# A decoder block on one core: the first expert pairs directly behind the routing choice, half of the embedding and the shared expert inside the first groups of four, a group of four at the end

## The chip, the core and the metric

The kernel runs on one core of one Trainium2 chip. The metric is the time of one execution on the device, in microseconds (us). TensorE is called PE in the profile (PEld is its weight load), VectorE DVE, ScalarE ACT, GpSimd POOL. SyncE (SP) issues nearly all loads; "SPq" is its queue.

## What is computed

One layer: 256 tokens of width 1024 go through two mixing branches (dilated attention and a gated recurrence) and a first norm, which gives `x1`. The change touches only what comes after that:

```python
idx, gate = route(h, w_router, bias)       # sigmoid scores, 4 of 8 expert groups, 8 of 64 experts per token
y_moe = (routed_experts(h, idx, gate, expert_w_gate, expert_w_up, expert_w_down)
         + swiglu(h, shared_w_gate, shared_w_up, shared_w_down))
ple = jax.nn.sigmoid(x1 @ ple_gate_w) * (p @ ple_proj_w)
x = layer_norm(ALPHA * x1 + y_moe + ple, ln2_w, ln2_b)
```

All 64 experts get some tokens, so all 64 sets of weights are read: three tiles of 128 x 2048 float32 (1 MB, 1,048,576 bytes) for each expert, 192 tiles in all. The embedding's gate weights (`pleg`) are four such tiles, the shared expert's gate and up (`shgu`) two, its down (`shd`) one.

## The kernel before, in words

**Stages.** Up to the first norm, PE works through the projections, the attention and the recurrence. Then (L596 to L620) `x1` is transposed and split in a high and a low part (`x1h`, `x1l`), and `dense` (L576) multiplies it with a weight in eight chunks of 128 rows. For each chunk ACT makes the high part of the weight, DVE the low part (`w2h`, `w2l`, W2 = 3 buffers of each), and PE does six matmuls of 512 columns.

**The choice.** The router's logits go through PE, ACT and then a chain of small DVE operations (L652 to L685) that ends in the mask `em`; `place` (L691) makes each token's slot (`posm`) of it with three matmuls and two DVE operations. While DVE works on this chain, PE runs `gated[0]` and `gated[1]`, the two halves of the embedding's gate (eight chunks each); DVE makes their low parts in between.

**Between the choice and the experts.** After `place`, PE runs the shared expert's gate and up (`shared`, eight chunks), and between the chunks come `add_emb` (L816, which puts the embedding and the residual into the accumulators `acc`) and the pieces of `rank` (L706), which orders the experts 8 to 63 by their load and writes the list `ids`. Experts 0 to 7 are in fixed order (FIXED = 8). SP reads `ids` before it loads any later expert (`expert_at`, L825).

**The experts.** `units` (L799) lists 13 units of two groups each. A group is a pair of experts (64 slots each) or four experts (32 slots each, the 24 experts with the fewest tokens; SMALL_AT = (2, 6, 9) says which units these are). For a group, PE gathers the tokens with a one-hot matrix `sel` (`unit`, `gather`, four steps for one unit's two groups, `xe`), multiplies with gate and up (tiles n = 0 and n = 1 of each expert), waits for `swiglu`, transposes `h`, multiplies with down (n = 2) and adds to `acc` (`scatter`). The gather steps of the next unit, and the second half of the scatter of the group before, are filled in between; two gather steps in each group.

**The ring.** All weight tiles go through a ring of slots of 1 MB (`slot`, L72), in order. RING_A 9, RING_B 6, RING_X 2 and the buffer of `x1` make 18; two more (RING_C) are added when the buffers of `dense` are given back, ahead of the first unit. A load waits until PE or DVE has read the tile that its slot held, and SP issues loads strictly in order, at most eight at a time in flight.

**The end.** The last unit's weights come in halves of 512 KB. Then the last norm (L1005) and the output.

PE's matmuls stand in the written order from L598 on (`fixed["pe"]`); DVE operations stand in it only where `late` holds them; the rest is ordered by the scheduler when the kernel is built.

Of the kernel before, what the change touches and what calls it, by code (L numbers as in the profile page):

```python
# [18 lines left out]
S = 256  # L19
# [3 lines left out]
NE = 64  # L23
# [9 lines left out]
WARM, YB, TB, W2 = 8, 2, 2, 3  # L33
FIXED, SMALL, SMALL_AT = 8, 24, (2, 6, 9)
# [3 lines left out]
RANK_AT = (1, 2, 3, 5)  # L38
# [18 lines left out]
def tile_block(ctx: ExitStack, tc: tile.TileContext, a, out: bass.AP):  # L57
# [50 lines left out]
    ple = ExitStack()  # L108
    ptg = ple.enter_context(tc.tile_pool(name="ptg", bufs=1))
# [304 lines left out]

    def gates():
        gp = transposed(next_win())
        t = ptg.tile([128, 2, S], F32, name="tg", bufs=4)
        act.activation(t, gp, AF.Tanh, scale=0.5)
        return t
# [97 lines left out]
    for f in range(2):  # L517
        if f:
            ps = [pmx.tile([128, 512], F32, name="ah", bufs=2) for _ in range(2)]
        else:  # L520
            ps = [ppj.tile([128, 512], F32, name="pj", tag="pj") for _ in range(2)]
        for i in range(2):
            for kt in range(2):
                whi, wlo = (w[f] for w in pws[kt])
                ts = slice(256 * kt + 128 * i, 256 * kt + 128 * i + 128)
                mm(ps[i], phi[:, ts], whi, start=kt == 0, stop=False)
                mm(ps[i], plo[:, ts], whi, start=False, stop=False)
                mm(ps[i], phi[:, ts], wlo, start=False, stop=kt == 1)
            emb[i][f] = ptg.tile([128, 512], F32, name="tg", bufs=4)
            act.activation(emb[i][f], ps[i], CP)  # L530
# [42 lines left out]
    load(rb, bcast(a["rbias"], NE))  # L573
    bd = ExitStack()
# [28 lines left out]
    wrh, wrl = (pbd.tile([128, KT * NE], F32R, name=n, tag=n, bufs=W2) for n in ("w2h", "w2l"))  # L603
# [16 lines left out]
    def ev_ple(f):  # L620
        def ev(i, ps):
            o = emb[i][f]
            act.activation(ps, ps, AF.Sigmoid)
            late(dve.tensor_mul(o, o, ps))
            late(dve.scalar_tensor_tensor(o, x1[:, i, 512 * f:512 * f + 512], ALPHA, o, op0=OP.mult, op1=OP.add))
        return ev

    gated = [dense([(raw(a["pleg"][2 * f + n]), 4) for n in range(2)], ev_ple(f),
                   [acc_bank() if f else bank("g") for _ in range(2)], (2, 0)[f]) for f in range(2)]
    sh_gu = [(raw(a["shgu"][n]), 4) for n in range(2)]  # L630
    sh_dn = raw(a["shd"])
    for kt in range(KT):
        if kt == ROUTER_SPLIT:
            next(gated[0])
# [5 lines left out]
    moved = act.activation(lgs, lg, CP)  # L640
    tr = bank("t", (128, 2, NE))
    next(gated[0])
    for i in range(2):
        pinned(pe.transpose(tr[:, i], lgs[:, 128 * i:128 * i + 128], ident[:NE, :NE]))
    act.activation(gate, tr, AF.Sigmoid)
    for f in range(2):
        for i in range(2):
# [3 lines left out]
            dve.tensor_sub(xl[:, i, c], x1[:, i, c], xh[:, i, c].bitcast(F32))  # L651
# [27 lines left out]
    dve.tensor_scalar(em, em, BIG, None, op0=OP.is_equal)  # L679
# [8 lines left out]
    for _ in gated[0]:  # L688
        pass

    def place():  # L691
# [9 lines left out]
        dve.tensor_scalar(posm, posm, NO_SLOT, None, op0=OP.add)  # L701
# [4 lines left out]
    def rank():  # L706


        t, t2 = (px2.tile([128, 512], F32, name="xs", bufs=2) for _ in range(2))
# [80 lines left out]
    nxe = count()  # L790

    def new_xe(shape):

        if next(nxe) % 6 < 2:
            return px2.tile(shape, F32, name="xe", tag="xs", bufs=2)
        return p3.tile(shape, F32, name="xe", bufs=4)
# [15 lines left out]


    acc = [[None, None], [None, None]]

    def add_emb(f):  # L816
        for i in range(2):
            hi, lo = (pbd.tile([128, 512], F32R, name=n, tag=n, bufs=W2) for n in ("w2h", "w2l"))
            act.activation(hi, emb[i][f], CP)
            late(dve.tensor_sub(lo, emb[i][f], hi.bitcast(F32)))  # L820
            acc[i][f] = acc_bank()
            for n, part in enumerate((hi, lo)):
                mm(acc[i][f], one, part, start=n == 0, stop=False)
# [30 lines left out]
    w0 = expert_weights(0, 2)  # L854
    ranking = rank()
    for kt in range(KT):
        next(gated[1])
    place()
    add_slots(pxx, 1, X_AT)
    s, xe, steps = unit(0)  # L860


    hs = None

    def ev_shared(i, ps):
        swiglu(hs[:, i], ps)

    shared = dense(sh_gu, ev_shared, [bank("g") for _ in range(2)])
    for kt in range(KT):
        if kt == 2:  # L870
            add_emb(0)
            hs = ptg.tile([128, 2, S], F32, name="tg", bufs=4)
        if kt == 4:
            add_emb(1)
        next(shared)
        if kt in RANK_AT:
            next(ranking)
    next(steps)
    next(steps)
    hT = bank("t", (128, 2, S))  # L880
    for i in range(2):
        for ft in range(2):
            transpose(hT[:, ft, 128 * i:128 * i + 128], hs[:, i, 128 * ft:128 * ft + 128])
    hth, htl = (ptg.tile([128, 512], F32R, name="tg", bufs=4) for _ in range(2))
    hTf = hT.rearrange("p f t -> p (f t)")
    act.activation(hth, hTf, CP)
    late(dve.tensor_sub(htl, hTf, hth.bitcast(F32)))
    gu0 = bank("g")
    gate_up(gu0, range(2), xe, 0, w0)
    for f in range(2):  # L890
        for ft in range(2):
            n = 2 * f + ft
            whi, wlo = split(pbd, sh_dn[:, 512 * n:512 * n + 512], 512, "w2", W2)
            for i in range(2):
                c = slice(256 * ft + 128 * i, 256 * ft + 128 * i + 128)
                for l, r in ((hth, whi), (htl, whi), (hth, wlo)):
                    mm(acc[i][f], l[:, c], r, start=False, stop=False)
    gate_up(gu0, range(2, 4), xe, 0, w0)
    fixed["pe"] = False
    bd.close()  # L900
    ple.close()
    for n in range(RING_C):
        add_ring(1, "left", f"ring_c{n}", C_AT[n])
    p2 = t2.enter_context(tc.tile_pool(name="p2", bufs=1, reuse_waits="tile"))
    p3 = t2.enter_context(tc.tile_pool(name="p3", bufs=1, reuse_waits="tile"))


    def experts(pl, bk, xe, off, s, gates, w, add, before=(), steps=(iter(()),) * 4, begun=None):
# [32 lines left out]
        for f in range(2):  # L941
            y = bk("g")
            for ft in range(2):
                for e in range(ne):
                    mm(y[sl * e:sl * e + sl], hT[:, ft, sl * e:sl * e + sl],
                       w[e][2][:, 1024 * f + 512 * ft:1024 * f + 512 * ft + 512], start=ft == 0, stop=ft == 1)
            yh = pl.tile([128, 512], F32R, name="yh", bufs=YB)
            yl = pl.tile([128, 512], F32R, name="yl", bufs=YB)
# [25 lines left out]
    for q, (r0, ne) in enumerate(units):  # L974
        if q + 1 < len(units):
            first = steps
# [9 lines left out]
        for pr in range(2):  # L986
# [3 lines left out]
            def add(i, f, l, halves, last=last):  # L990
                for n, r in enumerate(halves):
                    mm(acc[i][f], l, r, start=False, stop=last and n == 1)
                if last:
# [3 lines left out]
                           None if r else gu0)  # L997
# [41 lines left out]
    nr = nc.values_load(rounds[0:1, 0:1], min_val=1, max_val=S // SLOTS)  # L1039
    pair_no = px.tile([128, 1], F32, name="pair_no")  # L1040
    with tc.If(nr > 1):
# [7 lines left out]
        with tc.For_i(1, nr, 1):  # L1049
            dve.tensor_scalar(posm, posm, -float(SLOTS), None, op0=OP.add)  # L1050
            dve.memset(pair_no, 0.0)
            with tc.For_i(0, NE, 2) as c0:
                with tc.tile_pool(name="po", bufs=1) as po, \
# [38 lines left out]
                    for _ in experts(po, obank, xe, 0, s, lambda i: gp2[:, i], w, add):  # L1092
                        pass
# [109 lines left out]
```

## Time and profile before

| | us |
|---|---|
| time, median of 3 runs (906.29 to 907.25) | 906.7 |
| the profiled execution's own time | 905.45 |
| its span, first to last instruction | 903.7 |
| PE busy | 855.4 |
| mean granted PE clock, share of full speed | 0.989 |
| read from HBM | 268.85 MB |
| PE waiting for expert weights, 18 times after 450 us | 23.7 |

The span is cut in stretches, since it has different limits in them. Times in the text are us from the start of the span. The profiled execution lies 1.25 us under the median of the runs, and 1.75 us of it are outside the span.

### The profile page before, as it was taken

What the parts mean: (1) busy time and instruction counts of PE and PEld (TensorE: products, weight loads), DVE (VectorE), ACT (ScalarE), POOL (GpSimd) and SP (SyncE); (2) the same over time, 40 slices, a digit from 0 to 9 for tenths busy, and PEclk for the clock granted to TensorE, in tenths of its full rate; (3) what the DMA queues carried; (4) which work ended last, traced back from release to release, by engine and by line L of the source; (5) the groups of instructions that cost most, each with busy time, mean ns of one, the idle gap of its engine ahead of it and who ended that gap; (6) DMA issues with size and microseconds to landing.
All of it is one profiled execution on the core that took longest, in us unless ns stands there. A gap on an engine that the chain in (4) does not pass through costs nothing.

```text
span 903.7 us, 13958 instructions
## 1 busy us (share of the span) xinstructions
PE 855.4 (95%) x5200; PEld 564.9 (63%) x5200; DVE 377.9 (42%) x818; ACT 326.9 (36%) x651; POOL 154.0 (17%) x208
## 2 busy tenths in 40 slices
PE   9999999999999999899999999999689988899993
PEld 7899897888889999786545454544135433245431
DVE  5555555695966656897112122221012211112215
ACT  6444454566675545564212121221012211111221
POOL 0015463743400000302021011111011110101001
PEclk9999999999999999999999999999999998999997
DMA  9953433443334988454899999999999999999971
GB/s 334 421 216 131 141 99 135 150 141 129 121 137 158 363 306 305 172 199 141 322 386 417 413 421 420 421 419 422 420 420 422 420 420 422 421 421 420 405 311 49
DMA packets 42047, 270.84 MB, mean 300 GB/s; under 512 B 5060, under 2 KB 5188, under 8 KB 12280
## 3 DMA queue, kind: packets, MB, share of 16 engines
q1 hardware_dynamic: 41624, 269.20, 75.2%
q8 instruction: 42, 0.69, 0.3%
q10 hardware_dynamic: 288, 0.52, 0.2%
q0 software_dynamic: 64, 0.20, 0.1%
q14 instruction: 29, 0.24, 0.1%
HBM read 268.85 MB, written 1.05 MB: 299 GB/s over the span
## 4 chain that ended last, share of the span: by engine, by line
PE 62%; DMA 31%; DVE 5%; issue 1%; ACT 1%; SPq 0%; DVEq 0%
DMA raw<-in_exp_dram 30%; PE pj L103 26%; PE g L103 16%; PE acc L103 4%; PE ah L103 4%; PE t L103 4%; PE mix L472 2%; PE sc L103 2%; PE yp L103 1%; PE ap L381 1%; PE pt L260 1%; PE t L106 1%; DVE hr L365 1%; PE op L103 1%; DMA raw<-in_win_dram 0%
## 5 line engine op out<-in xcount | busy, mean ns | idle before, releaser
L103 PE MATMUL g<-raw,xe 128*64 128x512 f32 (+1 forms) x1024 | 204.4, 612 | 19.4 <-DMA raw<-in_exp_dram 19.4
L117 ACT ACTIVATE wh<-raw 128x512 fp32r<-128x512 f32 x213 | 132.3, 630 | 120.9 <-PE pj L103 86.2
L118 DVE TENSOR_TENSOR wl<-raw,wh 128x512 fp32r<-128x512 f32 x184 | 129.5, 715 | 90.7 <-ACT wh L117 69.9
L103 PEld LDWEIGHTS g<-raw,xe 128*64 128x64 f32 (+1 forms) x1024 | 60.3, 129 | 148.2 <-issue 110.3
L103 PE MATMUL pj<-xhi,wh 128*128 128x256 f32 x448 | 128.8, 288 | 0.2 <-DVE hq L366 0.2
L103 PE MATMUL pj<-xlo,wh 128*128 128x256 f32 x448 | 128.2, 286 | 0.0
L103 PE MATMUL pj<-xhi,wl 128*128 128x256 f32 x448 | 128.0, 286 | 0.0
L811 DVE TENSOR_TENSOR h<-h,g 128x256 f32<-128x256 f32 x52 | 21.9, 421 | 228.5 <-ACT h L809 227.6
L773 POOL TENSOR_SCALAR sel<-cst,posm 128x64 fp32r<-128x64 f32 (+1 forms) x120 | 47.3, 426 | 366.8 <-PE t L103 352.2
L103 PE MATMUL g<-raw,hT 128*64 128x512 f32 (+1 forms) x512 | 98.5, 598 | 4.9 <-DMA raw<-in_exp_dram 4.4
L809 ACT ACTIVATE h<-g 128x256 f32<-128x256 f32 x26 | 10.0, 385 | 222.4 <-PE g L103 222.4
L950 DVE SCALAR_TENSOR_TENSOR yl<-g,gsl,yh 128x512 fp32r<-128x512 f32 x52 | 39.0, 750 | 119.0 <-ACT yh L949 119.0
L103 PEld LDWEIGHTS pj<-xhi,wh 128*128 128x128 f32 x448 | 85.5, 191 | 3.5 <-issue 1.9
L103 PEld LDWEIGHTS pj<-xhi,wl 128*128 128x128 f32 x448 | 85.5, 191 | 3.1 <-issue 2.7
L103 PEld LDWEIGHTS pj<-xlo,wh 128*128 128x128 f32 x448 | 85.5, 191 | 2.7 <-issue 2.4
L118 POOL TENSOR_TENSOR wl<-raw,wh 128x512 fp32r<-128x512 f32 x29 | 38.5, 1337 | 156.7 <-ACT wh L117 146.7
L103 PEld LDWEIGHTS g<-raw,hT 128*64 128x64 f32 (+1 forms) x512 | 27.7, 126 | 56.9 <-issue 44.4
L949 ACT ACTIVATE yh<-g,gsl 128x512 fp32r<-128x512 f32 x52 | 35.8, 688 | 72.7 <-PE g L103 72.7
L103 PE MATMUL t<-sel,xh 128*128 128x256 f32 x208 | 56.1, 303 | 1.3 <-DVE gsl L930 1.3
L787 ACT ACTIVATE xe<-t 128x512 f32<-128x512 f32 x52 | 31.1, 598 | 68.8 <-PE t L103 68.8
L103 PEld LDWEIGHTS t<-sel,xh 128*128 128x128 f32 x208 | 39.2, 188 | 23.8 <-issue 22.7
L103 PE MATMUL t<-sel,xl 128*128 128x256 f32 x208 | 51.6, 281 | 0.0
(289 smaller groups left out, 1283.7 us busy)
## 6 DMA issues: line engine op xcount, KB each, us to landing
raw<-in_exp_dram SPq DMA_DIRECT2D x180, 1024.0 KB, 19.8
raw<-in_win_dram SPq DMA_DIRECT2D x40, 1024.0 KB, 5.2
raw<-in_exp_dram SPq DMA_DIRECT2D x24, 512.0 KB, 10.1
raw<-in_wab_dram SPq DMA_DIRECT2D x8, 768.0 KB, 4.7
raw<-in_wo_dram SPq DMA_DIRECT2D x4, 1024.0 KB, 8.1
raw<-in_pleg_dram SPq DMA_DIRECT2D x4, 1024.0 KB, 10.2
raw<-in_win_dram SPq DMA_DIRECT2D x8, 256.0 KB, 5.9
raw<-in_shgu_dram SPq DMA_DIRECT2D x2, 1024.0 KB
```

The costliest lines, as they stand in the source:

```text
L103: pinned(pe.matmul(o, l, r, start=start, stop=stop))
L106: pinned(pe.transpose(o, t, ident))
L117: act.activation(hi, src, CP)
L118: (lo_engine or dve).tensor_sub(lo, src, hi.bitcast(F32))
L260: pe.transpose(pt[:, b], pr[:, 128 * b:128 * b + 128], ident)
L472: ins = pe.matmul(mix[i][f], l[:, ts], r[f], start=j == n == 0, stop=j == 7 and n == 2)
L773: by.tensor_scalar(s[:, i, w * e:w * e + w], iota[:, 0:w], pos_of(i)[:, e:e + 1], None, op0=OP.is_equal)
L787: act.activation(xe[k2], ps, CP)
L809: act.activation(h, ps[:, 0:256], AF.Sigmoid)
L811: dve.tensor_mul(h, h, ps[:, 256 * n:256 * n + 256])
L949: act.activation(yh, y, CP, scale=gsl)
L950: dve.scalar_tensor_tensor(yl, y, gsl, yh.bitcast(F32), op0=OP.mult, op1=OP.subtract)
```

## The change

1. `gated[1]` (the embedding's second half) and `shared` leave the stretch between the choice and the experts. They become `late_embedding` and `late_shared`, called inside unit 2 (LATE_AT = 2, the first unit of groups of four), one behind each of its two groups. Their five tiles (two `pleg`, two `shgu`, one `shd`) are loaded there too, between the experts' tiles.
2. The first pair of experts starts right behind `place`: its one-hot, two gather steps, the first quarter of gate and up, and only then `add_emb` for the first half, and the pieces of `rank`.
3. `xh` and `xl` (the split of `x1` for the gathers) come later: `xh` behind the sigmoid of the gates, `xl` behind the mask and behind `posm`. The residual for the second half is read from `xh` and `xl`, since the buffer of `x1` has become a slot of the ring.
4. The chunks of `dense`, the parts for `add_emb` and the scratch of `rank` share the two buffers of `yh` and `yl`; the buffers `w2h` and `w2l` (three each) are gone. `xe` has four buffers in the first units instead of six. RING_C's two slots are added after unit 2. `late_shared` takes one slot of the ring as scratch (`keep`).
5. In units 0 and 1 the four gather steps for the next unit all stand in the second group; in unit 2 too.
6. SMALL_AT is (2, 7, 12): the last unit is now one of groups of four. In its very last group the second half of down goes expert by expert.
7. The load of `rounds` by SP comes behind the last weight load.

```diff
-WARM, YB, TB, W2 = 8, 2, 2, 3
-FIXED, SMALL, SMALL_AT = 8, 24, (2, 6, 9)
+WARM, YB, TB = 8, 2, 2
+FIXED, SMALL, SMALL_AT = 8, 24, (2, 7, 12)
...
-RANK_AT = (1, 2, 3, 5)
+LATE_AT = 2
...
+    def halves():
+
+        return (p2.tile([128, 512], F32R, name=n, bufs=YB) for n in ("yh", "yl"))
+
     def dense(chunks, evac, ps, pinned_kts=0):
...
-                whi, wlo = (pbd.tile([128, 512], F32R, name=n, tag=n, bufs=W2) for n in ("w2h", "w2l"))
+                whi, wlo = halves()
...
-    gated = [dense([(raw(a["pleg"][2 * f + n]), 4) for n in range(2)], ev_ple(f),
-                   [acc_bank() if f else bank("g") for _ in range(2)], (2, 0)[f]) for f in range(2)]
-    sh_gu = [(raw(a["shgu"][n]), 4) for n in range(2)]
-    sh_dn = raw(a["shd"])
+    emb0, gates0 = [], [bank("g") for _ in range(2)]
+    gated = dense([(raw(a["pleg"][n]), 4) for n in range(2)], sigmoid, gates0, 2)
...
+    def part_x(f, chosen):
+
         for i in range(2):
             c = slice(512 * f, 512 * f + 512)
             with tc.issue_after(moved.ins):
                 act.activation(xh[:, i, c], x1[:, i, c], CP)
-            dve.tensor_sub(xl[:, i, c], x1[:, i, c], xh[:, i, c].bitcast(F32))
+            with tc.issue_after(chosen.ins):
+                dve.tensor_sub(xl[:, i, c], x1[:, i, c], xh[:, i, c].bitcast(F32))
...
     w0 = expert_weights(0, 2)
+    part_x(0, chosen)
+    placed = place()
+    s, xe, steps = unit(0)
+    with tc.issue_after(placed.ins):
+        embed(0, gates0, emb0, x1)
+    part_x(1, placed)
+    add_slots(pxx, 1, X_AT)
+    gu0 = bank("g")
+    into = add_emb(0, emb0, True)
     ranking = rank()
...
     next(steps)
     next(steps)
...
     gate_up(gu0, range(2), xe, 0, w0)
...
+    for turn in (into, into, ranking):
+        next(turn)
     gate_up(gu0, range(2, 4), xe, 0, w0)
...
+    for turn in (ranking, steps, steps, ranking):
+        next(turn)
+
+
+    def late_embedding():
+
+        parts = []
+        gs = [bank("g") for _ in range(2)]
+        for _ in dense([(raw(a["pleg"][2 + n], ordered=True), 4) for n in range(2)], sigmoid, gs):
+            pass
+        embed(1, gs, parts, xh, xl)
+        return add_emb(1, parts, False)
+
+    def late_shared():
+        gu = [(raw(a["shgu"][n], ordered=True), 4) for n in range(2)]
+        dn = raw(a["shd"], ordered=True)
+        keep = slot(F32R)
...
-            for ft in range(2):
-                for e in range(ne):
...
+            turns = [(ft, e) for ft in range(2) for e in range(ne)]
+            for ft, e in sorted(turns, key=lambda t: t[1]) if final and f else turns:
...
-            if q == 0:
-                fill = ((list(first) for _ in (0,)), steps, steps, none), fill[1]
+            if q < LATE_AT:
+                fill = (none if q else ranking, none, none, none), (none, steps, steps, steps)
+            elif q == LATE_AT:
+                fill = (none,) * 4, (steps,) * 4
...
+            if q == LATE_AT:
+                for _ in rest:
+                    pass
+                rest = late_embedding() if pr == 0 else late_shared() or ()
...
+        if q == LATE_AT:
+            bd.close()
+            for n in range(RING_C):
+                add_ring(1, "left", f"ring_c{n}", C_AT[n])
+        for _ in steps:
+            pass
```

How the instructions moved, at three places. PE behind the slot positions: `t<-xs,cst` are the matmuls of `place`. Before, the shared expert's chunks follow (`w2h`, `w2l` against `x1h`, `x1l`):

```order
L103 MATMUL t<-xs,cst 128x64
L103 MATMUL t<-xs 128x64
L103 MATMUL t<-xs,cst 128x64
L103 MATMUL g<-w2h,x1h 128x512
L103 MATMUL g<-w2h,x1l 128x512
L103 MATMUL g<-w2l,x1h 128x512
```

Now the gathers follow (16 matmuls `t<-sel`); this is the end of them. `g<-raw,xe` is gate and up of the first pair, `acc<-yh,one` is `add_emb`, `t<-yh,rcols` begins `rank`:

```order
L103 MATMUL t<-sel_4603,xh 128x256
L103 MATMUL t<-sel_4603,xl 128x256
L103 MATMUL g<-raw,xe 64x512 x4
L103 MATMUL acc<-yh,one 128x512
L103 MATMUL acc<-yl,one 128x512
L103 MATMUL acc<-yh,one 128x512
L103 MATMUL acc<-yl,one 128x512
L103 MATMUL t<-yh,rcols 128x64 x2
L103 MATMUL t<-rcols,yh 64x1 x2
L103 MATMUL g<-raw,xe 64x512 x4
```

The first pair's gate and up now stand 16 gather matmuls behind `place`; before, the shared expert, `add_emb` for both halves and most of `rank` stood there.

SP's queue from the first norm's rows on, before (`TENSOR_LOAD cst` reads `ids`):

```order
L81 DMA raw<-in_ln1b_dram 128x1024
L81 DMA raw<-in_pleg_dram 128x2048 x4
L81 DMA raw<-in_shgu_dram 128x2048 x2
L81 DMA raw<-in_exp_dram 128x2048
L81 DMA raw<-in_shd_dram 128x2048
L81 DMA raw<-in_exp_dram 128x2048 x7
L81 DMA xs<-in_rbias_dram 128x64
L81 DMA raw<-in_exp_dram 128x2048 x8
L828 TENSOR_LOAD cst
```

and now:

```order
L81 DMA raw<-in_ln1b_dram 128x1024
L81 DMA raw<-in_pleg_dram 128x2048 x2
L81 DMA raw<-in_exp_dram 128x2048 x13
L81 DMA xs<-in_rbias_dram 128x64
L81 DMA raw<-in_exp_dram 128x2048 x7
L842 TENSOR_LOAD cst
```

Five tiles have left the front of the queue, and 20 expert tiles stand ahead of the reading of `ids`, where 16 stood.

PE in unit 2, at the end of its first group of four: before, gate and up of the second group follow the scatter at once:

```order
L103 MATMUL g<-raw,hT 32x512 x16
L103 MATMUL acc<-yh,sT 128x512
L103 MATMUL acc<-yl,sT 128x512
L103 MATMUL acc<-yh,sT 128x512
L103 MATMUL acc<-yl,sT 128x512
L103 MATMUL g<-raw,xe 32x512 x32
```

Now both halves of the scatter, and then 48 matmuls of the embedding's second half, of which the first three are shown:

```order
L103 MATMUL acc<-yh,sT 128x512
L103 MATMUL acc<-yl,sT 128x512
L103 MATMUL g<-yh,x1h 128x512
L103 MATMUL g<-yh,x1l 128x512
L103 MATMUL g<-yl,x1h 128x512
```

The embedding now stands between the two groups of unit 2; the shared expert stands in the same way behind the second group.

## Rows read from the trace of the kernel before

**Rows 1.** Page, part 2: GB/s moved in 40 slices of 22.6 us.

```profile
GB/s 334 421 216 131 141 99 135 150 141 129 121 137 158 363 306 305 172 199 141 322 386 417 413 421 420 421 419 422 420 420 422 420 420 422 421 421 420 405 311 49
```

**Rows 2.** Busy time by stretch: us, five engines, PEclk, DMA share, GB/s.

```profile
404.00:427.00 23.00, 20.95 (x109) 16.05 (x107) 17.80 (x52) 11.57 (x21) 5.40 (x11) 1.00 0.51 177
451.20:497.70 46.50, 46.50 (x235) 21.92 (x235) 9.18 (x22) 9.70 (x18) 8.68 (x24) 1.00 1.00 402
516.20:797.50 281.30, 256.80 (x1408) 113.36 (x1399) 47.76 (x115) 48.47 (x90) 30.71 (x80) 0.98 1.01 421
797.50:876.00 78.50, 78.47 (x374) 35.19 (x376) 15.41 (x35) 17.35 (x32) 3.33 (x8) 1.00 1.01 409
```

**Rows 3.** Waits of PE after 450 us: us in total, times, longest.

```profile
PE g L103 <- DMA raw<-in_exp_dram: 23.7, 18, 2.0
```

**Rows 4.** Chain that ended last, at its DMA links and end: start, us, what.

```profile
503.07 13.14 DMA raw<-in_exp_dram
...
777.73 19.75 DMA raw<-in_exp_dram
797.53 3.65 PE g L103 x14
...
873.88 7.02 PE g L103 x32
...
883.69 3.65 PE g L103 x16
```

**Rows 5.** Timeline of PE from the router to unit 2's second group: start, us.

```profile
385.81 0.33 PE L644 MATMUL t<-cst,xs 64*128 64x64 f32 x2
...
394.36 0.39 PE L103 MATMUL acc<-w2h,x1h 128*128 128x512 f32 x1
...
405.25 0.33 PE L103 MATMUL t<-xs,cst 128*128 128x64 f32 x2
...
451.20 7.09 PE L103 MATMUL g<-raw,xe 128*64 128x512 f32 x32
...
466.74 7.09 PE L103 MATMUL g<-raw,xe 128*64 128x512 f32 x32
...
497.70 7.07 PE L103 MATMUL g<-raw,xe 128*32 128x512 f32 x64
...
513.49 7.07 PE L103 MATMUL g<-raw,xe 128*32 128x512 f32 x64
```

**Rows 6.** Timeline of DVE: the choice's first step, `posm`, the first one-hot.

```profile
388.88 0.28 DVE L652 TENSOR_TENSOR xs<-xs 128x128 f32<-128x128 f32 x1
...
406.87 0.22 DVE L701 TENSOR_SCALAR posm<-posm 128x128 f32<-128x128 f32 x1
...
407.60 1.39 DVE L773 TENSOR_SCALAR sel<-cst,posm 128x64 fp32r<-128x64 f32 x8
```

**Rows 7.** DVE's largest groups, 388.88 to 407.09: count, busy us, mean ns, idle.

```profile
L584 DVE TENSOR_TENSOR w2l<-raw,w2h 128x512 fp32r<-128x512 f32 x14 | 9.5, 688 | 1.0 <-ACT w2h L583 0.7
L625 DVE SCALAR_TENSOR_TENSOR tg<-x,tg 128x512 f32<-128x512 f32 x3 | 2.0, 680 | 0.0
```

**Rows 8.** PE's groups in the shared expert's stretch, 405.83 to 424.93.

```profile
L103 PE MATMUL g<-w2h,x1h 128*128 128x512 f32 x16 | 6.6, 412 | 0.0
L103 PE MATMUL acc<-w2l,one 128*128 128x512 f32 x4 | 2.0, 500 | 1.6 <-DVE w2l L820 1.6
```

**Rows 9.** Timeline of PE: first and last of one gather step's eight matmuls.

```profile
520.49 0.39 PE L103 MATMUL t<-sel,xh 128*128 128x256 f32 x1
...
521.43 0.28 PE L103 MATMUL t<-sel,xl 128*128 128x256 f32 x1
```

**Rows 10.** DMA issues: count, KB each, median us from issue to landing.

```profile
raw<-in_exp_dram SPq DMA_DIRECT2D x180, 1024.0 KB, 19.8
...
raw<-in_exp_dram SPq DMA_DIRECT2D x24, 512.0 KB, 10.1
...
raw<-in_plep_dram SPq DMA_DIRECT2D x1, 1024.0 KB, 4.7
```

**Rows 11.** Timeline of SP, the last loads: start, us.

```profile
865.93 2.78 SPq L81 DMA_DIRECT2D raw<-in_exp_dram  x3
```

**Rows 12.** Timeline of PE in a group of four that waits for weights.

```profile
742.38 1.05 PE L103 MATMUL g<-raw,xe 128*32 128x512 f32 x2 [1.34 <-DMA raw<-in_exp_dram]
744.87 1.91 PE L103 MATMUL g<-raw,xe 128*32 128x512 f32 x2 [1.45 <-DMA raw<-in_exp_dram]
```

**Rows 13.** Busy time by stretch, around it (columns as in rows 2).

```profile
744.00:751.00 7.00, 5.55 (x22) 1.17 (x26) 0.00 (x0) 0.00 (x0) 0.00 (x0) 0.52 1.02 422
768.00:772.00 4.00, 4.00 (x24) 0.97 (x18) 0.00 (x0) 0.00 (x0) 0.00 (x0) 0.57 1.01 416
```

**Rows 14.** Page, part 5: the ACT operation of the splits.

```profile
L117 ACT ACTIVATE wh<-raw 128x512 fp32r<-128x512 f32 x213 | 132.3, 630 | 120.9 <-PE pj L103 86.2
```

More of the change, by code (lines that the diff above doesn't have):

```diff
@@ L602, in tile_block @@
     act.activation(one, ident, CP)
-    wrh, wrl = (pbd.tile([128, KT * NE], F32R, name=n, tag=n, bufs=W2) for n in ("w2h", "w2l"))
+    wrh, wrl = halves()
     act.activation(wrh, wr, CP)
@@ L618, in tile_block, with embed, sigmoid, add_emb @@
     lg = bank("t")[:NE, :S]
-    def ev_ple(f):
-        def ev(i, ps):
-            o = emb[i][f]
[L623 to L626, printed above, removed]
-    gated = [dense([(raw(a["pleg"][2 * f + n]), 4) for n in range(2)], ev_ple(f),
-                   [acc_bank() if f else bank("g") for _ in range(2)], (2, 0)[f]) for f in range(2)]
-    sh_gu = [(raw(a["shgu"][n]), 4) for n in range(2)]
-    sh_dn = raw(a["shd"])
+    acc = [[acc_bank() for _ in range(2)] for _ in range(2)]
+    def embed(f, gs, parts, *residual):
+        for i in range(2):
+            dve.tensor_mul(emb[i][f], emb[i][f], gs[i])
+        for i in range(2):
+            o = emb[i][f]
+            for x in residual:
+                dve.scalar_tensor_tensor(o, x[:, i, 512 * f:512 * f + 512].bitcast(F32), ALPHA, o,
+                                         op0=OP.mult, op1=OP.add)
+            hi, lo = halves()
+            act.activation(hi, o, CP)
+            dve.tensor_sub(lo, o, hi.bitcast(F32))
+            parts.append((hi, lo))
+    def sigmoid(i, ps):
+        act.activation(ps, ps, AF.Sigmoid)
+    def add_emb(f, parts, start):
+        for i in range(2):
+            for n, part in enumerate(parts[i]):
+                mm(acc[i][f], one, part, start=start and n == 0, stop=False)
+            yield
+    emb0, gates0 = [], [bank("g") for _ in range(2)]
+    gated = dense([(raw(a["pleg"][n]), 4) for n in range(2)], sigmoid, gates0, 2)
     for kt in range(KT):
         if kt == ROUTER_SPLIT:
-            next(gated[0])
+            next(gated)
         ws = slice(NE * kt, NE * kt + NE)
@@ L639, in tile_block @@
     lgs = scratch[0][:NE, :S]
-    moved = act.activation(lgs, lg, CP)
+    act.activation(lgs, lg, CP)
     tr = bank("t", (128, 2, NE))
-    next(gated[0])
+    next(gated)
     for i in range(2):
         pinned(pe.transpose(tr[:, i], lgs[:, 128 * i:128 * i + 128], ident[:NE, :NE]))
-    act.activation(gate, tr, AF.Sigmoid)
-    for f in range(2):
+    moved = act.activation(gate, tr, AF.Sigmoid)
+    def part_x(f, chosen):
         for i in range(2):
@@ L811, in swiglu @@
             dve.tensor_mul(h, h, ps[:, 256 * n:256 * n + 256])
[L814 to L823, printed above, removed]
     def expert_at(r):
@@ L854, in tile_block @@
     w0 = expert_weights(0, 2)
-    ranking = rank()
[L856 to L877, printed above, removed]
+    part_x(0, chosen)
@@ L885, in tile_block @@
[L885 to L888, printed above, removed]
-    gate_up(gu0, range(2), xe, 0, w0)
[L890 to L897, printed above, removed]
@@ L911, in experts @@
+    def experts(pl, bk, xe, off, s, gates, w, add, before=(), steps=(iter(()),) * 4, begun=None, final=False, halves=halves):
         ne, sl = len(w), 128 // len(w)
@@ L942, in experts @@
             y = bk("g")
-            for ft in range(2):
-                for e in range(ne):
[L945 to L948, printed above, removed]
+            turns = [(ft, e) for ft in range(2) for e in range(ne)]
+            for ft, e in sorted(turns, key=lambda t: t[1]) if final and f else turns:
+                mm(y[sl * e:sl * e + sl], hT[:, ft, sl * e:sl * e + sl],
+                   w[e][2][:, 1024 * f + 512 * ft:1024 * f + 512 * ft + 512], start=ft == 0, stop=ft == 1)
+            yh, yl = halves()
             act.activation(yh, y, CP, scale=gsl)
@@ L989, in tile_block, with add @@
             w = expert_weights(r, ne, q + 1 == len(units)) if r else w0
-            def add(i, f, l, halves, last=last):
+            def add(i, f, l, halves, first=not r, last=last):
                 for n, r in enumerate(halves):
-                    mm(acc[i][f], l, r, start=False, stop=last and n == 1)
+                    mm(acc[i][f], l, r, start=first and f == 1 and n == 0, stop=last and n == 1)
                 if last:
```

70 lines of the change are left out of this document (42 added, 28 removed).

## Prediction, made before the changed kernel ran

> **What bounds the kernel now.** I read the page's slices first. In slices 17 to 19 (360 to 430 us) the loads move 141 to 199 GB/s, from slice 22 to 38 405 to 422 [rows 1]. By stretch it is 177 GB/s in 404 to 427, 402 in the four pairs of units 0 and 1, 421 in 516 to 797 [rows 2]. A tile is 1,048,576 B, so at 421 GB/s it takes 2.49 us. PE waits 18 times for expert weights after 450 us, 23.7 us in all [rows 3]. The chain of waits says the same in time: from 503.07 to 797.48 it runs through loads (fourteen links of some eight tiles, of which the first and the last are shown), behind that through PE to the end [rows 4]. Over the first 281 us behind 516.2 it makes 2.51 us a tile with the short pauses in it, which I use.
>
> The timeline of PE gives what a group costs. A pair of experts takes 15.5 us (451.20 to 466.74) and reads six tiles, 15.1 us of loading: PE sets the pace by a hair. A group of four takes 15.8 us (497.70 to 513.49) and reads twelve tiles, 30.1 us: the loads set it [rows 5]. So the kernel has an idle memory before about 450 us, since the 18 slots are full and PE frees none of them, and from 500 us on a full one. What brings the second pair forward, and with it the freeing of slots, ends the kernel earlier; what puts PE work beside the groups of four is free there as long as slots still come free in time.
>
> **The choice.** The change takes 48 matmuls out of the stretch before the slots are known, 394.36 to 405.25, 10.9 us (0.227 each), and then the shared expert's stretch [rows 5]. DVE is what ends the choice: it starts at 388.88 and writes `posm` at 406.87, 18 us later [rows 6]. In these 18 us it is busy 9.5 us with 14 low parts of the dense chunks, and some 4.5 with seven operations on `tg` of 0.68 each (three are in the row) [rows 7]; that leaves 4.0 us for the choice itself, or 6.5 if only the three of the row fall in it. Now four low parts (2.8 us) stand there and half of `xl` (two, 0.8). The two buffers instead of three hold the router's parts longer and delay the logits by about 1.2 us, but the sigmoid is no longer behind `xh` on ACT; I start the choice at 388.4. With 7.5 us for its own operations (above the larger value, since small ones wait for each other) `posm` is there at about 399.5, where it was 407.1. Then stand two products and two sums for the embedding, the second half of `xl`, and the one-hot of 1.39 [rows 6]: first gather at about 403.6, against 424.9. Nothing covers PE between about 398 and 403.6; that idle time is in the count.
>
> **The first pair.** Its matmuls cost one pair, 15.5. To this come two more gather steps (the eight matmuls of one run from 520.49 to 521.43 and a little, 0.95 us [rows 9]), 1.9; the pieces of `rank` and `add_emb`; and `swiglu` with the transposes, which now has less to cover it, 1.6. For `rank`, `add_emb` and the hand-overs the trace has only the shared expert's stretch, 405.83 to 424.93: 19.1 us less the 10.9 of 48 matmuls leaves 8.2 as the upper bound; the row of four `add_emb` matmuls shows 2.0 us of work and 1.6 of waiting [rows 8], and four of the eight are left, so that 2.0, with no wait and nothing for `rank`, is the lower bound. I take 4.7: the row with its wait, 3.6, and 1.1 for the pieces of `rank`. Second pair at 403.6 + 15.5 + 1.9 + 4.7 + 1.6 = 427.3, where it was 451.20: a lead of 23.9 us.
>
> `ids` follows `rank`, at about 414.6. SP's four reads of it hold up all loads queued behind, but the next slots come free when the first pair's gate and up are through, at about 419, so this wait costs nothing; if `ids` came 10 us later it would begin to.
>
> **Units 0 and 1.** The gather steps stand together in the second group: 15.5 + 1.9, then 13.6 + 0.8 for an uncovered `swiglu`, then 17.4 again, 49.2 us where the same stretch took 46.5 [rows 5]. Unit 2 starts at 476.5, before at 497.70: the lead is down to 21.2.
>
> **The stream of loads.** Here most of the lead goes. Five tiles that were loaded before the choice, where the slices show 306 GB/s and less [rows 1], are now in the full stream: 5 x 2.51 = 12.5 us. The ring has 18 slots instead of 20 until the end of unit 2, two tiles less in stock, 5.0 us. Counted through: in the first four pairs the ring is full and PE sets the pace. By 475.4 PE has freed 22 tiles, so 40 have been loaded; the next load is issued then and takes 4.7 us alone, as the one lone 1 MB load did [rows 10]: 480.1. From there the stream need not stop. 192 + 5 = 197 tiles, 156 of them still to come: 480.1 + 156 x 2.51 = 871.7. The last 48 loads are halves, where 24 were; the last 78 us of before ran at 409 instead of 421 GB/s, which bounds this at 2.2 us; I take 0.6, since PE's freeing accounts for part of that. Last landing 872.3. Before, the last issue at about 868.4 [rows 11] and the 10.1 us of a half [rows 10] make 878.5: 6.2 us earlier.
>
> **Unit 2.** The moved work is 120 matmuls of 0.227, 27.2 us, and hand-overs, transposes, splits and two scatters that can't be filled in. Bounds: nothing, and twice the 8.2 of above, so 27.2 to 43.6; I take 38. Unit 2 ends at 476.5 + 2 x 15.8 + 38 = 546. The loads go on beside it until the ring is full again, at tile 53 + 18: 480.1 + 30 x 2.51 = 555 at the most, 550 with the slot that the shared expert holds as scratch. There are 4 to 9 us of slack; beyond that each us counts. Afterwards nine units stand before the last (two groups each, 15.5 or 15.8 us [rows 5]): PE is at the last unit at about 826, when 5 of its 24 tiles have landed, and does not wait for weights before.
>
> **The tail.** Before, the last six groups are pairs and PE is late: the last y ends at 883.69 + 3.65 = 887.3 [rows 4], 8.8 us behind the last landing. Now the last unit is one of groups of four. PE waits there for the loads, and after the last one only two pairs of matmuls stand, 2 x 1.05 us, at most 2 x 1.91 [rows 12]. From the end of y to the end of the span it took 903.7 - 887.3 = 16.4; the statistics of the first half are done earlier, -0.7. End: 872.3 + 2.1 + 16.4 - 0.7 = 890.1, 13.6 below 903.7. Of it 6.2 come from the loads, the rest from the tail. The load of `rounds` falls where SP only waits for the outputs: nothing. The profiled execution (905.45) lies 1.25 below the median, so I take the difference from the median: 906.7 - 13.6 = **893.1**.
>
> **The rivals.** (A) *Moved work in series, slower.* With two buffers instead of three, a chunk in unit 2 could cost the sum of its steps: ACT 0.63 [rows 14], DVE 0.69 [rows 7] and six matmuls 1.37, 2.7 us instead of 1.37. 16 chunks make +21 us; less the slack of 4 to 9 that is 12 to 17 us on the stream, and with the same in the choice the time is 905 to 910. It takes the whole gain when the moved work costs about 58 us instead of 38. Against it: two buffers alternate, and 0.63 + 0.69 is below 1.37, so that the split of one chunk fits beside the matmuls of the other. Chance 0.13.
>
> (B) *The clock.* [...] Chance 0.18. [...]
>
> (C) *First pair later.* `rank` at its upper bound (8.2 instead of 4.7), or the operations of the choice waiting for each other longer: +3.5 to +8, 897 to 901. For it: PE's order is fixed, and the second quarter of gate and up stands behind a piece of `rank` that needs DVE. Only if the second pair began after 441 us would the whole gain be gone. Chance 0.13.
>
> (D) *More gain.* `rank` at its lower bound and a quicker choice: 886 to 890. Chance 0.08.
>
> That the order is not what the text of the change says is out: PE's rows and SP's queue show it as described.
>
> **How the numbers follow.** The forecast, 889 to 897, has 0.48, and 893 is its middle. About 0.2% (1.8 us) is what a measurement of this kernel tells from no change. The range of 886 to 903 holds the forecast, B, C and most of D and leaves out most of A, some 0.16. Of A, 0.04 lies within 0.2% of 906.7 and 0.09 above it; all else is faster, 0.87.
>
> **What would show it.** The first one-hot near 403, gate and up of the second pair at 427 and of the first group of four at 476; `ids` read near 415; 410 GB/s or more from 480 to 870, with no hole near 545; chunks in unit 2 spaced 1.4 us (A: 2.4 or more); unit 3 at 546; long waits for weights in the last unit, with its granted clock (B); last landing 872, span 890. I am wrong if the second pair starts behind 441, or if the loads sag between 500 and 560.

## The result, and the profile after

| | predicted | measured |
|---|---|---|
| time, median (first four runs, 895.79 to 897.88) | 893.1, range 886 to 903 | 896.34 |
| ratio to before (906.98 in these runs) | 0.985 | 0.9885, 95% interval 0.9867 to 0.9902 |
| slot positions (`posm`) | 399.5 | 397.6 |
| first gather | 403.6 | 400.86 |
| second pair's gate and up | 427.3 | 427.19 |
| first group of four | 476.5 | 476.59 |
| unit 3 | 546 | 546.72 |
| last landing | 872.3 | 877.0; 874.1 in a second profile |
| end of the last y (the result of the last down matmuls) | 874.4 | 878.9; 876.0 |
| span | 890.1 | 895.7; 892.9 |

The change gains 10.6 us where 13.6 were forecast. The first profiled execution took 897.88 us, the longest of its four; a second one of the same kernel, further down as `after_again`, took 895.02. For the end of the kernel the table gives both.

The GB/s line of the page (40 slices), the answer to [rows 1]:

```profile
GB/s 334 420 222 136 141 96 141 151 139 134 94 134 155 363 326 285 157 170 235 364 367 395 422 420 421 420 420 422 419 421 419 420 421 423 420 421 386 410 394 58
```

Slices 19 and 20 (403 to 448) have risen from 141 and 322 to 235 and 364. Slice 22 is lower than before, 395 instead of 417: the ring is now short there. Busy time by stretch (columns as in [rows 2]):

```profile
401.00:404.00 3.00, 3.00 (x14) 2.91 (x15) 2.89 (x7) 1.75 (x3) 1.91 (x3) 0.50 0.26 35
...
421.00:427.00 6.00, 6.00 (x20) 1.94 (x16) 0.82 (x2) 1.38 (x2) 0.00 (x0) 0.72 0.59 250
427.00:476.50 49.50, 48.63 (x252) 23.89 (x250) 9.93 (x22) 10.41 (x19) 8.65 (x24) 1.00 0.98 385
476.50:546.00 69.50, 65.18 (x384) 39.53 (x383) 27.79 (x51) 23.46 (x40) 3.32 (x8) 0.95 1.00 412
546.00:797.00 251.00, 250.06 (x1354) 116.48 (x1354) 49.94 (x116) 51.72 (x96) 30.54 (x80) 1.00 1.01 421
```

From 476 to 546, where the moved work stands, the loads run on at 412 GB/s, and to 797 at 421, with PE busy 250 of 251 us. The granted clock is 0.50 behind the idle stretch ahead of the first gathers, and 0.72 on average in 421 to 427. It falls a third time inside the moved work: ahead of the shared expert's down PE waits three times (0.70, 0.95 and 0.69 us, from 534.8 to 538.0), and the clock is 0.65 on average behind that, while the loads go on at 422 GB/s:

```profile
540.00:546.00 6.00, 6.00 (x19) 4.68 (x19) 1.39 (x2) 1.26 (x2) 0.00 (x0) 0.65 1.01 422
```

So the moved work is longer than it need be; how much of the slack beside the loads this takes, no run measures.

PE's timeline at the places that the prediction named (start, us):

```profile
400.86 0.55 PE L103 MATMUL t<-sel,xh 128*128 128x256 f32 x1 [3.96 <-DVE sel L799]
...
420.79 5.35 PE L103 MATMUL g<-raw,hT 128*64 128x512 f32 x16 [0.52 <-DVE hT L955]
...
427.19 7.09 PE L103 MATMUL g<-raw,xe 128*64 128x512 f32 x32
...
476.59 7.07 PE L103 MATMUL g<-raw,xe 128*32 128x512 f32 x64
...
546.72 7.09 PE L103 MATMUL g<-raw,xe 128*64 128x512 f32 x32
```

PE waits 3.96 us for the one-hot. The first pair's down (16 matmuls) takes 5.35 us, against 3.65 for the same matmuls in the chain of before [rows 4]. PE's waits after 380 us, and the end of the chain of waits:

```profile
PE t L103 <- DVE sel L799: 4.0, 1, 4.0
PE g L103 <- DMA raw<-in_exp_dram: 3.5, 14, 0.5
```

```profile
826.07 3.57 PE g L103 x32
830.42 10.10 DMA raw<-in_exp_dram
...
861.01 11.01 DMA raw<-in_exp_dram
872.07 6.82 PE g L103 x26
```

Waiting for weights is down from 23.7 us [rows 3] to 3.5, and it all stands in the last unit, from 826 us on, as forecast. The loads are links of the chain only there; ahead of 826 us PE is the chain, running even with them.

### The profile page after: what moved, and what is told of

Same layout as the page of the kernel before. It is cut to its first block, busy times and chain, and to the rows that moved or that the text cites. A ratio compares the mean times of both kernels' runs of the same rounds, so it can differ in the third digit from the quotient of the medians.

```text
span 895.7 us, 14001 instructions
## 1 busy us (share of the span) xinstructions
PE 857.5 (96%) x5200; PEld 566.0 (63%) x5200; DVE 380.4 (42%) x820; ACT 327.5 (37%) x651; POOL 154.3 (17%) x208
## 4 chain that ended last, share of the span: by engine, by line
PE 85%; DVE 6%; DMA 5%; ACT 1%; issue 1%; SPq 0%; DVEq 0%; ACTq 0%
PE g L103 33%; PE pj L103 26%; PE t L103 8%; PE acc L103 6%; DMA raw<-in_exp_dram 5%; PE ah L103 4%; PE mix L473 2%; PE sc L103 2%; PE yp L103 1%; PE ap L380 1%; PE t L106 1%; DMA raw<-in_xt_dram 1%; PE pt L259 1%; DVE hr L364 1%; PE op L103 1%
## 5 line engine op out<-in xcount | busy, mean ns | idle before, releaser
L103 PE MATMUL g<-raw,xe 128*64 128x512 f32 (+1 forms) x1024 | 196.9, 596 | 3.3 <-DMA raw<-in_exp_dram 2.5
L103 PEld LDWEIGHTS g<-raw,xe 128*64 128x64 f32 (+1 forms) x1024 | 57.2, 126 | 126.2 <-issue 108.8
L103 PE MATMUL g<-raw,hT 128*64 128x512 f32 (+1 forms) x512 | 103.1, 605 | 3.1 <-DVE hT L955 2.1
## 6 DMA issues: line engine op xcount, KB each, us to landing
raw<-in_exp_dram SPq DMA_DIRECT2D x168, 1024.0 KB, 15.7
```

Of the source, the lines that this page charges most:

```text
L103: pinned(pe.matmul(o, l, r, start=start, stop=stop))
```

## Experiments: how the gain divides

First the two parts of the change, each alone.

**Order of the groups alone**, in the kernel before:

```diff
-FIXED, SMALL, SMALL_AT = 8, 24, (2, 6, 9)
+FIXED, SMALL, SMALL_AT = 8, 24, (2, 7, 12)
```

> The kernel before with one edit: SMALL_AT is (2, 7, 12), so that its last unit is one of groups of four. Nothing else is moved. Theory (the tail has a gain of its own): before, the last y ended 8.8 us behind the last landing, since six pairs stood at the end; with a group of four there it ends some 2 us behind it. 48 loads in halves instead of 24 cost 1 to 2 us of that. Expected 901.5 us (900 to 903). Rival (the end can only move when the loads start earlier): 906 to 908, the last y about 8 us behind the last landing.

Measured: 900.9 us, ratio 0.9934 (0.9913 to 0.9955). PE's weight loads and matmuls at the end:

```profile
881.43 0.16 PEld L103 LDWEIGHTS g<-raw,hT 128*32 128x32 f32 x8 [1.12 <-DMA raw<-in_exp_dram]
```

```profile
881.43 1.90 PE L103 MATMUL g<-raw,hT 128*32 128x512 f32 x10 [0.21 <-DMA raw<-in_exp_dram]
```

The last half lands at 881.4. In the kernel before, the last packet of the loads ends at 878.4 by the trace's DMA records, here at 880.9, so the loads end 2.5 us later; yet the last y ends 1.9 us behind the last landing, at 883.3 instead of 887.3. The tail has a gain of its own, 5.5 us, with no early pair. In it is the price of 24 more loads in halves.

**All but the order**, in the changed kernel, with SMALL_AT back at (2, 6, 9):

> The changed kernel with one edit: SMALL_AT is (2, 6, 9) again, so that six pairs stand at the end. Theory (the early first pair moves the stream of loads by little, since five tiles and two slots eat most of its lead): last landing near 875.5 instead of 878.5, PE as late behind it as before, expected 903 us (902 to 904.5). Rival (the early pair is the whole gain): 896 to 898.

Measured: 901.21 us, ratio 0.9947 (0.9930 to 0.9965), 1.8 us better than expected and 0.8 below the interval. PE's last y is again a pair's:

```profile
877.74 3.70 PE L103 MATMUL g<-raw,hT 128*64 128x512 f32 x16 [0.52 <-DVE hT L955]
```

The last y ends at 881.4. In this trace the last packet of the loads ends at 873.4, so the last y ends 8.0 us behind it, about as late as before (887.3 and 878.4, 8.9). The expectation had been made from the last landing of the first profile of after; with 24 halves the loads end 5.0 us earlier than before. The prediction had 6.2, with 0.6 for 24 more halves in it, so 6.8 for this kernel. 906.4 - 900.9 = 5.5 and 906.4 - 901.2 = 5.2 make 10.7: the two parts add up to the 10.6 of the whole change, and neither needs the other. How the 5.2 divides between the earlier pair, the later order of the loads and the other edits of that part was not tested one by one.

## Experiments: what the moved work costs

**Neither loaded nor computed** (the two calls for the late work are left out):

```diff
-                rest = late_embedding() if pr == 0 else late_shared() or ()
+                rest = ()
```

> The changed kernel without the moved work: the embedding's second half and the shared expert are neither loaded nor computed (so the residual and the embedding of half the width, and the shared expert, are missing from the output). Theory (the stream of loads is the bound, five tiles of 2.5 us in it): 12.5 us less than the changed kernel's 896.3, 884 us (882 to 886). Rival A (the moved PE work is on the path as well): 878 or less. Rival (PE is the bound and the tiles are hidden): as the kernel with loads alone.

Measured: 882.68 us, 13.9 below the changed kernel (896.6, the median of its eight runs in two sets).

**Loaded, not computed** (the five tiles are loaded at the same places and never read):

> The changed kernel with the five moved tiles loaded at their places, but nothing computed from them (the embedding's second half, its residual and the shared expert are missing from the output). Theory (the moved PE work lies beside the loads): the time stays that of the changed kernel, 896.3 us (895 to 897.5). Rival A (the work is on the path): 885 to 892, lower by what of its 38 us isn't hidden.

Measured: 895.18 us, ratio 0.9876 (0.9856 to 0.9896), 1.4 below the changed kernel. So five tiles cost 895.2 - 882.7 = 12.5 us, five times 2.5, and the PE work on them, with the slot that `late_shared` takes as scratch, 1.4 by the medians. That rules out the rival of serial work on the path. In the trace of the changed kernel the 48 matmuls of the embedding stand without a gap from 492.63 to 503.8, 1.40 us a chunk.

**More work in the same place** (n matmuls whose result isn't used, ahead of the embedding's second half; n = 48, then 96):

```diff
         gs = [bank("g") for _ in range(2)]
+        for _ in range(n):
+            mm(gs[0], x1h[:, 0, :128], xh[:, 0, 0:512])
```

> The changed kernel with 48 more matmuls (result not used) ahead of the embedding's second half in unit 2, 11.1 us more of PE work there. Theory (beside the loads there is a slack, not an endless one: a tile is issued at 544.8 that must be issued by about 551.5 if the loads are not to run dry, 6.7 us): 4.4 us above the changed kernel, 900.8 (899 to 902.5), loads with a hole of 4 to 5 us near 520 to 555. Rival (all PE work in unit 2 is hidden): 896.5. Rival A (the work there is on the path): 907.

> As the one before, with 96 more matmuls, 22.3 us, which is the +21 us that the prediction's rival A set on serial chunks. Theory (one to one beyond 6.7 us of slack): 15.6 us above the changed kernel, 912 (909.5 to 914), so slower than the kernel before. Rival (hidden): 896.5; rival A (no slack): 918.

Measured: 902.84 (ratio 0.9963, 0.9952 to 0.9974) and 914.92 (1.0094, 1.0078 to 1.0109), which is 6.2 and 18.3 us above the changed kernel for 11.1 and 22.3 us of PE work. The slack is 11.1 - 6.2 = 4.9 or 22.3 - 18.3 = 4.0 (12.1 us of time for the second 11.2 us of work): at the lower end of the 4 to 9 of the prediction, and below the 6.7 that I had read from one load. Both values lie outside the expected intervals by 0.3 and 0.9 us. Where the loads ran dry, with 48 more (busy time by stretch):

```profile
505.00:515.00 10.00, 9.30 (x44) 7.24 (x42) 4.87 (x8) 4.32 (x7) 0.00 (x0) 1.00 0.81 318
515.00:530.00 15.00, 14.85 (x126) 7.08 (x130) 6.21 (x14) 4.33 (x8) 3.32 (x8) 1.00 0.83 329
...
545.00:560.00 15.00, 12.44 (x47) 7.38 (x48) 4.13 (x8) 2.66 (x5) 0.00 (x0) 0.89 0.93 365
```

I had taken the slack at the load of 544.8 us; the tighter place is 30 us earlier. Against the 418 to 422 GB/s of the changed kernel in the same stretches, the first two rows lose some 5.6 us of loading and the third 2.0. While PE works on the embedding it gives a tile back once in four chunks, 5.6 us (loads are issued at 496.78 and 502.38 in the changed kernel), and the stream wants one every 2.5. The ring lives on its stock there. The price of work beyond the slack is about one to one, as the prediction said, and 96 more matmuls make the kernel slower than before. So rival A had the price right; the serial chunks that were to bring the extra work did not come (1.40 us a chunk). The whole gain would be gone some 15 us of PE work above what the change does (the gain of 10.6 and the slack of 4 to 4.9).

## Experiments: the idle stretch and the clock

The changed kernel once more, beside the next three:

> The changed kernel itself once more, so that the next three are compared with it on the same chip. Expected 896 us (895 to 897.5); its last landing 2 to 3 us before the 877.0 of the first profile, if the two slips of 1.5 us in the landings there belong to that execution and not to the kernel.

Measured: 897.11 us, ratio 0.9902 (0.9886 to 0.9918). The profiled execution's last weight load that waits for a tile:

```profile
874.13 0.14 PEld L103 LDWEIGHTS g<-raw,hT 128*32 128x32 f32 x2 [0.25 <-DMA raw<-in_exp_dram]
```

It stands at 876.99 in the first profile of the changed kernel. The 2.9 us belong to the execution. The second pair begins at 426.72 here.

**Idle matmuls ahead of the first gathers**:

```diff
     ranking = rank()
+    for _ in range(32):
+        mm(acc[0][1][:, :256], x1h[:, 0, :128], x1h[:, 0])
     next(steps)
```

> The changed kernel with 32 matmuls of 256 columns, whose result isn't used, between the slot positions and the first gathers, where PE is idle for 4 us. Theory (the idle stretch puts PE at half clock, and the 16 gather matmuls behind it take 3.7 us instead of 1.9; the second pair and with it the stream of loads are late by that): gathers at 0.12 us a matmul, second pair 1.8 us earlier, time 1.8 us below the changed kernel (1 to 2.5). Rival (the clock there costs nothing in the end, since the ring's stock of tiles covers it): same time, the first tile of the full stream at 480 us as before.

Measured: 894.49 us, ratio 0.9874 (0.9856 to 0.9892), 2.1 below the eight runs of the changed kernel, 2.6 below the four beside it. Timeline of PE, and busy time by stretch:

```profile
396.63 4.08 PE L103 MATMUL acc<-x1h 128*128 128x256 f32 x32
...
424.19 7.09 PE L103 MATMUL g<-raw,xe 128*64 128x512 f32 x32
```

```profile
401.00:404.00 3.00, 2.91 (x20) 2.13 (x21) 2.57 (x6) 2.01 (x4) 1.85 (x3) 1.00 0.19 33
```

The clock is 1.00 where it was 0.50, gate and up begin 2.4 us behind the first gather instead of 3.65, and the second pair at 424.19 instead of 427.19. That is more than the 1.2 us between them, since the first pair's down now takes 3.65 us as well. Against `after_again`, and counted from the matmuls of `place`, the second pair comes 1.9 us earlier. In the nine traces of kernels with the early pair and without idle matmuls that down took 5.35 us in five and 3.65 in four (`after_again` is one of these; there the first eight matmuls of gate and up take 2.37 us instead of 1.94): the half clock there comes and goes. At the gathers it was there in all nine.

**The embedding's products behind `xl`**:

> The changed kernel with DVE's two products for the embedding behind the second half of xl instead of ahead of it, so that the first one-hot comes 1.3 us earlier. Theory (what DVE does between the slot positions and the one-hot is on the path to the end, one to one): 1.3 us below the changed kernel (0.7 to 1.8), first gather near 399.6. Rival (the first pair then waits for the embedding's parts instead): same time, second pair again at 427.

Measured: 896.53 us, ratio 0.9894 (0.9879 to 0.9909), no difference. The edit did not do what it was for. DVE's timeline:

```profile
397.29 1.29 DVE L676 TENSOR_TENSOR xl<-x,xh 128x512 fp32r<-128x512 f32 x2
398.50 1.28 DVE L632 TENSOR_TENSOR tg<-tg,g 128x512 f32<-128x512 f32 x2
399.69 1.68 DVE L800 TENSOR_SCALAR sel<-cst,posm 128x64 fp32r<-128x64 f32 x8
```

`xl` and the products have changed places, and the one-hot still stands behind both. This run tells nothing about the theory; the last experiment puts it right.

## Experiments: the halves, and a faster kernel

**24 halves**, in the changed kernel, only the last group's:

```diff
-            w = expert_weights(r, ne, q + 1 == len(units)) if r else w0
+            w = expert_weights(r, ne, last) if r else w0
```

> The changed kernel with loads in halves only for the very last group, 24 as before, instead of 48. Theory (a half costs 1.28 us where half a tile costs 1.24, and the first group of the last unit gains nothing from halves): landings between 814 and 845 at 2.49 us a tile, last landing 1 us earlier, time 0.5 to 1.5 us below the changed kernel, 895.5. Rival (the first group then starts late and hands its delay on): same or up to 2 us above.

Measured: 894.74 us, ratio 0.9869 (0.9854 to 0.9884), 1.9 below the changed kernel, a little more than expected. The size is loose: the profiled executions of the two kernels (895.29 here, 895.02 in `after_again`) don't show it, and the last landing here is not earlier (875.1 against 874.1). The stretch 814 to 845, here and (second fence) in the second profile of the changed kernel:

```profile
814.00:845.00 31.00, 27.40 (x158) 10.69 (x158) 4.97 (x14) 5.69 (x11) 0.00 (x0) 1.00 1.01 418
```

```profile
814.00:845.00 31.00, 30.29 (x171) 11.51 (x168) 5.72 (x15) 6.53 (x13) 0.00 (x0) 1.00 1.02 404
```

Whole tiles come at 418 GB/s, halves at 404, with the DMA engines as busy.

**Five edits together** (the 32 idle matmuls, 12 more behind the first pair's gate and up, the embedding's products behind `xl`, 24 halves, and the first half's statistics behind the last low part of y on DVE):

> The changed kernel with five edits together: 32 idle matmuls ahead of the first gathers; 12 behind the first pair's gate and up, where PE waits 1.9 us for h; the embedding's products behind xl; loads in halves only for the very last group (24 instead of 48); and the first half's statistics behind the last low part of y. If each is worth what the changed kernel's rows give (1.8, 1.7, 1.3, 1.0 and 0.5 us), 6.3 us below the changed kernel (4 to 7), about 890. Rival (PE's pace early on isn't what sets the stream): 1 to 2 us below, from the halves and the statistics alone.

Measured: 890.67 us, ratio 0.9834 (0.9819 to 0.9848), 5.9 below the changed kernel. PE's waits:

```profile
PE t L106 <- DVE h L838: 0.7, 2, 0.4
PE acc L103 <- DVE yl L969: 0.5, 2, 0.3
```

The wait for the one-hot is gone from the list, since the idle matmuls fill it, and that for `yl` is 0.5 instead of the 1.0 of the changed kernel.

**The one-hot first**: the same, with the one-hot directly behind `posm` on DVE, then `xl`, then the embedding, and 16 idle matmuls:

> The kernel with five edits once more, with the first one-hot directly behind the slot positions on DVE, then the second half of xl, then the embedding (before, the embedding's products still stood ahead of the one-hot), and 16 idle matmuls instead of 32. Theory (DVE's stretch ahead of the one-hot is on the path): first gather near 399.0 instead of 400.9; the embedding's parts then make PE wait about 1 us, so second pair 0.8 us earlier (0.3 to 1.8), time 890 (889 to 891). Rival (PE waits as long for the embedding's parts as it gained): second pair at 424.2 again, 890.7.

Measured: 889.86 us, ratio 0.9821 (0.9808 to 0.9835). PE's timeline:

```profile
397.86 2.16 PE L103 MATMUL acc<-x1h 128*128 128x256 f32 x16
399.86 0.28 PE L103 MATMUL t<-sel,xh 128*128 128x256 f32 x1
...
423.61 6.66 PE L103 MATMUL g<-raw,xe 128*64 128x512 f32 x30
```

The slot positions came 1.2 us later in this execution (`place` at 397.28 instead of 396.12), and still the first gather is 1.0 earlier than in the changed kernel; the second pair is 0.6 earlier than in the trace of five edits (423.61 against 424.25). The time is 0.8 less, as expected, but at this size the runs alone don't tell it from no difference. It is the fastest kernel of this study that computes everything, 6.7 us below the changed one.

## Why the prediction was right, and where it was not

**The views led to the right bound.** That the loads from 480 us on set the end, that PE's work beside the groups of four is free up to a limit, and that six pairs at the end were a loss of their own: each has a run of its own now (12.5 us for five tiles, 1.4 us for 38 us of PE work, 5.5 us for the order). The forecast's sum of 6.2 from the loads and 7.4 from the tail stands against 5.2 and 5.5 measured, with the price of the added halves in the first term there and in the second here. The sum is 3.0 us too large, and the terms below are why.

**The lead was right by two errors, which is luck.** The second pair is at 427.19, forecast 427.3. But the first gather came 2.7 us sooner than I had it (400.86 instead of 403.6). Of this 1.2 us are the start: I began the choice at 388.4, and DVE's row for its first step is at 387.17, so the logits did not pay the 1.2 us that I set for two buffers. The choice itself took 0.7 less. The last 0.8 lie between `posm` and the gather, where my 4.1 us did not hold what I listed. DVE's rows there:

```profile
397.50 1.28 DVE L632 TENSOR_TENSOR tg<-tg,g 128x512 f32<-128x512 f32 x2
398.69 1.37 DVE L676 TENSOR_TENSOR xl<-x,xh 128x512 fp32r<-128x512 f32 x2
399.98 1.38 DVE L799 TENSOR_SCALAR sel<-cst,posm 128x64 fp32r<-128x64 f32 x8
401.28 1.33 DVE L636 SCALAR_TENSOR_TENSOR tg<-x,tg 128x512 f32<-128x512 f32 x2
```

Products, `xl`, one-hot and sums make 5.4 us, and the two sums (L636) stand behind the one-hot, not ahead of it. Two operations on `xl` take 1.3 us, where I had 0.8. The way from the first gather to the second pair took 26.3 us instead of 23.7, because gathers and down ran at half clock (0.50 in 401 to 404 and in 422 to 424), 1.2 and 1.7 us more. My sum had the idle time ahead of the gathers in it, but not the clock behind it: 0.50 behind 3.96 us of waiting here, 1.00 with idle matmuls in the same place (`e3_warm`). In the last unit the clock did not fall:

```profile
846.00:862.00 16.00, 14.56 (x63) 3.25 (x56) 0.75 (x1) 1.28 (x2) 0.00 (x0) 1.00 1.03 410
862.00:872.00 10.00, 8.32 (x38) 2.25 (x33) 1.80 (x7) 0.77 (x2) 0.00 (x0) 1.00 1.02 404
```

PE waits some 0.2 us at a time there, 0.5 at the most, before a pair of matmuls or a few, and keeps 1.00; it is idle 3.1 of 26 us. Waits as long as those of [rows 12], in the group whose clock [rows 13] give, did not come. That the clock would fall in the last unit was my estimate, and the two profiles of the changed kernel do not show it; in `e4_24_halves` it is 1.00 in 814 to 845, in `e10_hot_first` 0.94 on average.

**The terms that were mis-sized**, against the second profile (892.9 instead of 890.1). The last landing is 1.8 late. Of this the halves are the term that a run has measured: 1.9 us for 24 more of them by the times, 1.0 by the rates (12.6 MB at 404 instead of 418 GB/s), where I took 0.6 with 2.2 as the bound, and gave as the reason that PE's freeing accounted for the slower rate in the last 78 us of before. It was the halves, which begin at 842 us there:

```profile
834.00:843.00 9.00, 9.00 (x45) 4.13 (x45) 2.24 (x5) 2.16 (x4) 0.00 (x0) 1.00 1.01 421
848.00:860.00 12.00, 12.00 (x62) 5.99 (x61) 3.08 (x7) 2.91 (x6) 0.00 (x0) 1.00 1.01 395
860.00:868.00 8.00, 8.00 (x32) 2.99 (x30) 1.58 (x5) 1.85 (x4) 0.00 (x0) 1.00 1.01 383
```

I also said that the stream need not stop from 480.1 on; four tiles were issued at 480 only, and in the first profile the 43rd tile, the first of them, landed 4.6 us behind the one before it (in the second 2.7). From the end of y to the end of the span it takes 16.8 us, not 15.7: I took 0.7 off because the first half's statistics are done earlier, and they stand on DVE just ahead of the last low part, for which PE then waits 0.7 us. In the run with that order mended (five edits) this wait is 0.3. The last 0.4 us lie outside the span: 1.75 us of a profiled execution before, 2.1 to 2.2 now, and I had taken the difference of the spans for that of the times.

**The rivals.** A (serial) is out for this kernel: chunks of 1.40 us. Its threshold was put at 58 us of moved work; by the runs it is 38 and 15, so about 53. B (the clock) is right for the first pair (0.50 at its gathers and in its down) and not for the last unit (1.00). Of C little came: `ids` was written at 413.6, forecast 414.6, SP was through with its four reads at 416.1 and the next slot came free at 418.0; the longer way to the second pair is accounted for by the clock. Of D the quicker choice came, and the clock ate it.

## What to carry to other kernels

Where a stream of loads sets the end, count in tiles: what was loaded early for nothing and must now pass through the full stream has its full price (2.5 us each here), and what PE does beside the stream is free only until the ring has run dry (4 to 4.9 us of slack here), which came first here where PE held its tiles longest (one given back in 5.6 us). Put groups that wait for loads last and groups that PE paces ahead of them (5.5 us here). When a change opens an idle stretch on PE ahead of work on the path, look at the granted clock behind it as well (0.50 behind 4 us of waiting here), and try matmuls that nobody reads in it (1.00 with them, and 2.1 us less).

## What was not expected

In the stretches shown above halves of 512 KB moved at 383 to 410 GB/s, by stretch and execution (346 in 814 to 820 of the first profile of the changed kernel), where tiles of 1 MB moved at 418 to 421, though the DMA engines show as busy (1.00 to 1.03, and 1.01): 3% and more.

Landings slip by up to 1.5 us now and then: in the first profile of the changed kernel between 507.41 and 511.43, where the stream wants one tile each 2.5 us, and again near 700; in other executions they are smaller or elsewhere. The bytes don't stop there. In the first of these stretches the whole queue moves 417 GB/s, and one packet of the instruction queue falls in it, which takes 0.8% of 16 engines for 9 us, so about 1.1 us of one engine:

```profile
DMA packets 510, 3.75 MB, mean 417 GB/s; under 512 B 53, under 2 KB 53, under 8 KB 53
q8 instruction: 1, 0.02, 0.8%
```

Such a packet stands in the stretch near 700 as well. But they come about every 25 us (20 of them in 400 to 875), mostly without a slip, so that they make the slips is not shown, and the cause stays open. Of the 2.9 us between the last landings of the two profiles of the changed kernel they are the smaller part: by the landings that the traces record, 1.6 us are there at the first tile issued at 480 (487.53 against 485.93), 2.1 from 514 to 702, and the rest comes in the halves.
